# State weights from planes repeated by DMA and formed turned on VectorE, in place of transposes on TensorE

## The chip, the cores and the metric

The kernel runs on one core of one Trainium2 chip. The metric is the time of one execution in microseconds of the device; lower is better. Times are given as the median of several runs; a profiled execution gives the span from the first to the last instruction.

## The reference, cut to what matters

The layer normalises x (512 tokens, 1024 channels), multiplies it by one wide matrix (8192 columns are used here in the parts u, z, q, k, v and two gates), runs a state-space branch (S5) and an attention branch, and merges them. The change is in the S5 branch:

```python
dt = jnp.exp(log_dt.astype(f32))[:, None]
mag = jnp.exp(lr * dt)
ab_re = mag * jnp.cos(li * dt)
ab_im = mag * jnp.sin(li * dt)
den = lr * lr + li * li
nr = ab_re - 1.0
f_re = (nr * lr + ab_im * li) / den
f_im = (ab_im * lr - nr * li) / den
bb_re = f_re[..., None] * br - f_im[..., None] * bi
bb_im = f_re[..., None] * bi + f_im[..., None] * br
...
    bu_re = jnp.einsum('blgp,gnp->blgn', u_c, bb_re)
    bu_im = jnp.einsum('blgp,gnp->blgn', u_c, bb_im)
    pa_re, pa_im, hs_re, hs_im = lax.associative_scan(
        _complex_diag_combine, (a_re, a_im, bu_re, bu_im), axis=1)
```

There are 64 groups with 64 states (n) and 16 channels (p, called q in the kernel). A state is h(t) = a h(t-1) + f b u(t), where a, f and b are complex.

## The kernel before

**Tiling of S5.** The 512 tokens stand as 64 runs of T = 8. For each run and state the kernel needs the sum over the 8 tokens k of a^(7-k) f b u(k). That is a matmul whose contraction goes over the 128 pairs (k, q); its weights W have (k, q) on the partitions and the 64 states of two groups on the columns. Groups are taken in eight batches j of eight groups. W of one batch is 128 x 1024 values: real and imaginary part, eight groups, 64 states.

**How W comes about (lines 434 to 448).** VectorE forms a^k (tile AT) times f b (tile BB) with the states on the partitions, in six operations of 128x512 for each j (`coef`, called twice). Eight transposes of 128x128 on TensorE (`wps`) turn it so that (k, q) lies on the partitions, and two copies of ScalarE bring it from PSUM to W. `x_unit(j)` then multiplies W with the tokens Uj in 32 small matmuls (`xps`) and ScalarE copies the result to Xs.

**Coefficients (lines 514 to 606).** VectorE computes exp, sine and cosine on 64 partitions (groups) with 64 states. Then pw holds the powers a^1 to a^8 and f. `f_turn` turns f by 8 small matmuls (`ftp`) to the layout with states on partitions; GpSimd (into tb) and VectorE make BB = f b from D1, the loaded b. `a_turn` turns the powers by 64 small matmuls (`atp`) into AT.

**After W.** A scan on VectorE runs over the batch results (`scan_work`, tile scn). `ca_coef(j)` forms c a^k on VectorE (six operations of 128x576), `m_unit(j)` multiplies it with BB on TensorE (`kps`), ScalarE copies the result to kt, GpSimd adds the skip and stores kt with eight DMAs in the matrix M. `chunk(j)` computes the output of batch j (`yps` from M, the tokens, the states and ca), then turns it (`yT`) and applies GELU.

**What fills TensorE.** All projections are sums of three matmuls on a high and a low part (`mm3`), in units of 24 matmuls of 128x512 (`cm_unit`, tile pj). Weights are loaded on SyncE's queue, split by ScalarE (w_hi) and VectorE (w_lo).

**What sets the order.** TensorE's instructions have the order in which the program calls them (`follow`, lines 62 to 74). The other engines' order is made by a scheduler of the compiler from a timeline that it simulates, in which an instruction may be placed ahead of others that the program names earlier; `tc.issue_after(ins)` holds an instruction behind another on its engine. The S5 work is placed between projection matmuls by a list of events (lines 939 to 954): each has a block number, and a block is six projection matmuls. Blocks 0 to 19 are the units u(3) to u(7), 20 to 35 za, 36 to 67 zs, then v0, v, rs and ra up to 119.

```python
W0, K0B, V0B, Y0 = 16, 49, 74, 88
```

**Rooms.** Big tiles share places by a tag: s1 is dd (D1, BB and the three M), s5 is abt (the products of `coef`), s6a and s6b the two W, s7a and s7b pw and tq, later kt.

Of the kernel before, what the change touches and what calls it, by code (L numbers as in the profile page):

```python
# [52 lines left out]
def tile_hybrid_block(ctx: ExitStack, tc: tile.TileContext, x, positions, norm_w, w_in, lam_re, lam_im,  # L53
# [382 lines left out]

    def w_unit(j):
        ba = ab[j % 2][:, 0:8 * T * Q].rearrange("p (a g k q) -> p a g k q", a=2, g=4, k=T)
        p4 = slice(4 * j, 4 * j + 4)
        for a in range(2):  # L440
            coef(ba[:, a], 4 * j, BB[:, 1 + a, p4], BB[:, a, p4], 1, T + 1, ab[2][:, 512 * a:], dve)
        W = big.tile([P, 8, P], F32, name="W", tag=("s6a", "s6b")[j % 2])
        for h in range(2):
# [3 lines left out]
            act.copy(W[:, 4 * h:4 * h + 4].rearrange("p g n -> p (g n)"), ps)
        return W
# [98 lines left out]
    dve.tensor_tensor(pw[:, 1, 8], t1, den, op=ALU.mult)
    tq = big.tile([G, 2, 4, N], F32, name="tq", tag="s7b")
    for n in (1, 2, 4):

        br_ = pw[:, 0:1, n - 1:n, :].broadcast_to([G, 2, n, N])
# [4 lines left out]
        dve.tensor_tensor(tq[:, :, 0:n], a, bi_, op=ALU.mult)
# [22 lines left out]
    tb = ab[0][:, 0:1024].rearrange("p (a g q) -> p a g q", a=2, g=H)  # L579
    def f_turn():  # L580
        pf = bank("ftp")
        for i in range(2):
            for h in range(2):
                pe.matmul(pf[64 * h:64 * h + 64, i * H:(i + 1) * H], pw[:, i, 8], idg[:, h], start=True, stop=True,
                          skip_group_check=True)
        act.copy(fT.rearrange("p a g -> p (a g)"), pf[:, 0:2 * H])
        pool.tensor_tensor(tb, D1, fi, op=ALU.mult)
        dve.tensor_tensor(BB[:, 1:3], D1, fr, op=ALU.mult)
        dve.tensor_tensor(BB[:, 2], BB[:, 2], tb[:, 0], op=ALU.add)
        dve.tensor_tensor(BB[:, 1], BB[:, 1], tb[:, 1], op=ALU.subtract)  # L590
        act.activation(BB[:, 0], BB[:, 2], AF.Copy, scale=-1.0)

    def a_turn():
        ps = bank("atp")
        for i in range(2):
            for k in range(8):
# [799 lines left out]
```

## Time and profile before

| | before |
|---|---|
| median of 3 runs | 679.34 us (678.24 to 680.03) |
| profiled execution, its time | 678.55 us |
| its span | 676.5 us |
| granted clock of TensorE | 1.000 |
| DMA packets and bytes | 137380, 82.13 MB |

The page gives, for each engine, the busy time, its share of the span and the number of instructions. Waits are given as engine, line and tile that waited, then what released it, the total in us, how many times, and the longest. The timeline gives start, duration, engine, line, operation, what is written and read, and a count where equal instructions were merged; the duration of a merged row is that of the whole group. In groups of instructions the numbers behind the first bar are the busy sum in us and the mean of one in ns.

### The profile page before, as it was taken

The numbers are of one execution on the slowest core, as the hardware profiler recorded it, in microseconds if no ns is written. First come the engines' busy times: TensorE is split into PE (matmuls) and PEld (weight loads), VectorE is DVE, ScalarE is ACT, GpSimd is POOL, SyncE is SP. The second block draws the span as 40 slices with busy tenths as digits, with TensorE's granted clock in tenths as the row PEclk, the third lists the DMA queues.
The fourth block names the chain that finished last, engine by engine and source line by source line (L and its number), as shares of the span: only waits on it lengthen the run. The fifth ranks groups of instructions, "written<-read, shape, count | busy, mean of one in ns | idle before, by whom it ended". The sixth has DMA issues, their size and how long they took to land.

```text
span 676.5 us, 12719 instructions
## 1 busy us (share of the span) xinstructions
PE 669.5 (99%) x4841; PEld 565.3 (84%) x4841; DVE 465.3 (69%) x964; ACT 322.5 (48%) x677; POOL 118.2 (17%) x274
## 2 busy tenths in 40 slices
PE   8999999999999999999999999999999999999997
PEld 7988888889888888878889888888888888888886
DVE  7989879999788365863238777658566856667531
ACT  6644552423467663431344674557456745633210
POOL 1020000600365329510000030012001200220000
PEclk9999999999999999999999999999999999999999
DMA  9665425552566543573332423222222213237231
GB/s 307 134 164 146 122 55 146 148 167 85 156 141 147 148 148 107 155 249 94 93 107 81 140 63 95 62 63 74 84 83 74 72 55 94 94 134 286 94 125 62
DMA packets 137380, 82.13 MB, mean 121 GB/s; under 512 B 32736, under 2 KB 125928, under 8 KB 137192
## 3 DMA queue, kind: packets, MB, share of 16 engines
q1 hardware_dynamic: 134968, 78.31, 39.2%
q0 software_dynamic: 2048, 2.36, 2.2%
q8 instruction: 38, 0.62, 0.4%
q10 hardware_dynamic: 304, 0.66, 0.3%
q14 instruction: 22, 0.18, 0.1%
HBM read 68.46 MB, written 10.49 MB: 117 GB/s over the span
## 4 chain that ended last, share of the span: by engine, by line
PE 92%; DVE 4%; issue 2%; ACT 1%; DMA 1%; POOL 0%; ACTq 0%; DVEq 0%; POOLq 0%
PE pj L69 76%; PE sps L69 3%; PE yps L69 2%; PE ot L69 2%; PE ptp L74 2%; PE qtp L74 2%; PE xps L69 1%; DVE gth L1258 1%; DVE w_lo L252 1%; PE wps L74 1%; ACT w_hi L250 1%; DMA x_all<-in_x_dram 1%; PE kps L69 1%; PE yT L74 1%; PE cps L69 0%
## 5 line engine op out<-in xcount | busy, mean ns | idle before, releaser
L250 ACT ACTIVATE w_hi<-w_raw 128x1024 fp32r<-128x1024 f32 x94 | 99.4, 1059 | 162.0 <-PE pj L69 132.2
L252 DVE TENSOR_TENSOR w_lo<-w_raw,w_hi 128x1024 fp32r<-128x1024 f32 x94 | 117.1, 1247 | 66.3 <-ACT w_hi L250 65.3
L69 PE MATMUL pj<-hT_hi,w_hi 128*128 128x512 f32 (+1 forms) x344 | 131.8, 385 | 0.0
L69 PE MATMUL pj<-hT_lo,w_hi 128*128 128x512 f32 (+1 forms) x344 | 128.8, 376 | 0.4 <-DVE hT_lo L355 0.4
L69 PE MATMUL pj<-hT_hi,w_lo 128*128 128x512 f32 (+1 forms) x344 | 126.8, 375 | 0.0
L69 PE MATMUL pj<-w_hi,hT_hi 128*128 128x512 f32 (+1 forms) x288 | 108.7, 377 | 0.0
L69 PE MATMUL pj<-w_hi,hT_lo 128*128 128x512 f32 (+1 forms) x288 | 105.6, 367 | 0.0
L69 PE MATMUL pj<-w_lo,hT_hi 128*128 128x512 f32 (+1 forms) x288 | 105.5, 366 | 0.0
L69 PEld LDWEIGHTS pj<-hT_hi,w_hi 128*128 128x128 f32 x344 | 64.7, 188 | 13.1 <-issue 1.3
L69 PEld LDWEIGHTS pj<-hT_lo,w_hi 128*128 128x128 f32 x344 | 64.8, 188 | 11.1 <-DVE hT_lo L355 0.6
L69 PEld LDWEIGHTS pj<-hT_hi,w_lo 128*128 128x128 f32 x344 | 63.7, 188 | 12.0
L69 PEld LDWEIGHTS pj<-w_hi,hT_lo 128*128 128x128 f32 x288 | 54.3, 189 | 9.1
L69 PEld LDWEIGHTS pj<-w_hi,hT_hi 128*128 128x128 f32 x288 | 54.4, 189 | 8.5 <-issue 0.5
L69 PEld LDWEIGHTS pj<-w_lo,hT_hi 128*128 128x128 f32 x288 | 54.5, 189 | 7.5
L1120 POOL COPY sw<-st 32x4 f32<-32x4 f32 x64 | 11.9, 185 | 175.0 <-ACT Pt L1076 172.2
L1021 DVE SCALAR_TENSOR_TENSOR qkp<-qtp,wcol,qkp 128x512 fp32r<-128x512 f32 (+1 forms) x32 | 23.6, 748 | 25.3 <-ACT qkp L1020 25.2
L1076 ACT ACTIVATE Pt<-Pt,st 128x256 f32<-128x256 f32 (+1 forms) x64 | 30.9, 484 | 19.8 <-DVE st L1074 19.8
L845 POOL DMA_DIRECT2D dd<-kt x64 | 33.8, 536 | 2.4 <-POOL kt L841 2.1
L1020 ACT ACTIVATE qkp<-qtp,wcol 128x512 fp32r<-128x512 f32 (+1 forms) x32 | 21.2, 683 | 23.0 <-PE qtp L74 20.8
L69 PE MATMUL pj<-w_lo,mT_hi 128*128 128x512 f32 (+1 forms) x72 | 26.3, 366 | 0.0
L69 PE MATMUL pj<-w_hi,mT_hi 128*128 128x512 f32 (+1 forms) x72 | 26.3, 366 | 0.0
L69 PE MATMUL pj<-w_hi,mT_lo 128*128 128x512 f32 (+1 forms) x72 | 26.3, 365 | 0.0
(301 smaller groups left out, 1189.6 us busy)
## 6 DMA issues: line engine op xcount, KB each, us to landing
w_raw<-in_w_in_dram SPq DMA_DIRECT2D x36, 512.0 KB
w_raw<-in_w_in_dram SPq DMA_DIRECT2D x112, 128.0 KB
w_raw<-in_w_glu_dram SPq DMA_DIRECT2D x8, 512.0 KB
w_raw<-in_w_ssm_out_dram SPq DMA_DIRECT2D x8, 512.0 KB
w_raw<-in_w_o_dram SPq DMA_DIRECT2D x8, 512.0 KB
w_early<-in_w_in_dram SPq DMA_DIRECT2D x4, 512.0 KB
ud<-uT SPq DMA_DIRECT2D x8, 256.0 KB
uss<-ud SPq DMA_DIRECT2D x8, 256.0 KB
```

The costliest lines, as they stand in the source:

```text
L69: last[0] = nc.tensor.matmul(*a, **k)
L74: last[0] = nc.tensor.transpose(*a, **k)
L250: last_act[0] = act.activation(hi, raw, AF.Copy).ins
L252: dve.tensor_tensor(lo, raw, hi.bitcast(F32), op=ALU.subtract)
L845: pool.dma_start(M[Q * t:Q * t + Q, :, 0:P - Q * t], kt[:, :, t:].rearrange("q g k p -> q g (k p)"))
L1020: act.activation(hi, ps[sl], AF.Copy, scale=w)
L1021: dve.scalar_tensor_tensor(lo, ps[sl], w, hi.bitcast(F32), op0=ALU.mult, op1=ALU.subtract)
L1076: act.activation(o, o, AF.Exp, bias=nm, scale=-1.0, accum_out=st[:, kind, 1, h, b:b + 1])
L1120: pool.tensor_copy(sw[32 * r:32 * r + 32, :, :, b], st[32 * b:32 * b + 32, 1, :, :, r])
L1258: dve.scalar_tensor_tensor(th, th, 1.0, z, op0=ALU.add, op1=ALU.mult)
```

## The change

W is no longer turned on TensorE. The products a^(7-k) f are formed on 64 partitions (tile pf, eight rows k), stored to DRAM (pfd), and read back so that each row k of a batch, 1024 values in 4 KB, is repeated on the 16 partitions of its q. b is turned once by eight transposes (`b_turn`), stored (btd), and read back with each row q repeated for the 8 rows k. Both planes then lie as W does, and `w_unit` is four operations of VectorE: two of 128x1024 and two of 128x512. All these DMAs are issued on GpSimd's queue: two stores, and sixteen loads of 512 KB. `f_turn` also turns a; `a_powers` forms the powers with states on the partitions on VectorE, and `a_turn` goes. tb is made on VectorE in place of GpSimd. BB loses its third, negated part. The planes lie in parts of abt and dd, two sets. The two old events of w and x work are parted: `w_next(j)` from block 12 on, `x_unit(j)` from block 15 on, both 3.5 blocks apart. `ca_coef(2)` moves from block 41 to 90, behind the scan. The first chunk moves from block 88 to 90, and chunks are 10/3 in place of 11/3 blocks apart.

```diff
+    def load_planes(j):
+        PB = planes[j % 2]
+        pool.dma_start(PB[0], bass.AP(pfd.tensor, pfd.offset + 1024 * j, [(2 * G * N, T), (0, Q), (1, 1024)]))
+        pool.dma_start(PB[1], bass.AP(btd.tensor, btd.offset + 1024 * j, [(0, T), (2 * H * P, Q), (1, 1024)]))
+        PBs[j] = PB
+
     def w_unit(j):
-        ba = ab[j % 2][:, 0:8 * T * Q].rearrange("p (a g k q) -> p a g k q", a=2, g=4, k=T)
-        p4 = slice(4 * j, 4 * j + 4)
-        for a in range(2):
-            coef(ba[:, a], 4 * j, BB[:, 1 + a, p4], BB[:, a, p4], 1, T + 1, ab[2][:, 512 * a:], dve)
+        PB = PBs.pop(j)
         W = big.tile([P, 8, P], F32, name="W", tag=("s6a", "s6b")[j % 2])
-        for h in range(2):
-            ps = bank("wps")
-            for g in range(4):
-                pe.transpose(ps[:, g * P:(g + 1) * P], ba[:, h, g].rearrange("p k q -> p (k q)"), ident)
-            act.copy(W[:, 4 * h:4 * h + 4].rearrange("p g n -> p (g n)"), ps)
+        Wv = W.rearrange("p m n -> p (m n)").rearrange("p (a g n) -> p a g n", a=2, n=N)
+        pl = PB[0].rearrange("p (g a n) -> p a g n", a=2, n=N)
+        bl = PB[1].rearrange("p (a g n) -> p a g n", a=2, n=N)
+        br, bi = (bl[:, i:i + 1].broadcast_to([P, 2, 8, N]) for i in range(2))
+        dve.tensor_tensor(Wv, pl, br, op=ALU.mult)
+        dve.tensor_tensor(pl, pl, bi, op=ALU.mult)
+        dve.tensor_tensor(Wv[:, 0], Wv[:, 0], pl[:, 1], op=ALU.subtract)
+        dve.tensor_tensor(Wv[:, 1], Wv[:, 1], pl[:, 0], op=ALU.add)
+        if j + 2 < 8:
+            load_planes(j + 2)
         return W
...
-    W0, K0B, V0B, Y0 = 16, 49, 74, 88
+    W0, K0B, V0B, Y0 = 16, 49, 74, 90
...
+    def times(o, a, br_, bi_, t):
         dve.tensor_tensor(o, a, br_, op=ALU.mult)
-        dve.tensor_tensor(tq[:, :, 0:n], a, bi_, op=ALU.mult)
...
+        dve.tensor_tensor(t, a, bi_, op=ALU.mult)
+        dve.tensor_tensor(o[:, 0], o[:, 0], t[:, 1], op=ALU.subtract)
+        done[0] = dve.tensor_tensor(o[:, 1], o[:, 1], t[:, 0], op=ALU.add).ins
+
+    done = [None]
+    tq = big.tile([G, 2, T - 1, N], F32, name="tq", tag="s6b")
+    for n, m in ((1, 1), (2, 2), (4, 3)):
+        e = T - 1
+        sh = [G, 2, m, N]
+        times(pw[:, :, e - n - m:e - n], pw[:, :, e - m:e], pw[:, 0:1, e - n:e - n + 1].broadcast_to(sh),
+              pw[:, 1:2, e - n:e - n + 1].broadcast_to(sh), tq[:, :, 0:m])
+    sh = [G, 2, T - 1, N]
+    times(pf[:, :, 0:T - 1], pw[:, :, 0:T - 1], f1[:, 0:1].unsqueeze(2).broadcast_to(sh),
+          f1[:, 1:2].unsqueeze(2).broadcast_to(sh), tq)
+    pf_done = done[0]
+    pfd = dram.tile([T, G, 2 * N], F32, name="pfd")
+    pool.dma_start(pfd.rearrange("k g m -> g k m"), pft.rearrange("g k a n -> g k (a n)"))
...
-    tb = ab[0][:, 0:1024].rearrange("p (a g q) -> p a g q", a=2, g=H)
+    tb = dd[:, 1024:2048].rearrange("p (a g q) -> p a g q", a=2, g=H)
+    planes = [(abt[:, 3072:4096], dd[:, 2048:3072]), (dd[:, 0:1024], dd[:, 1024:2048])]
...
+    def b_order():
+        for i in range(2):
+            act.copy(dd[:, 1024 + 512 * i:1536 + 512 * i].rearrange("p (m j q) -> p m j q", m=4, q=Q),
+                     D1[:, i].rearrange("p (j m) q -> p m j q", m=4))
+
+    def b_turn():
+        bt = dd[:, 2048:3072]
+        for i in range(2):
+            ps = bank("btp")
+            Dv = dd[:, 1024 + 512 * i:1536 + 512 * i].rearrange("p (m c) -> p m c", m=4)
+            for m in range(4):
+                pe.transpose(ps[:, m * P:(m + 1) * P], Dv[:, m], ident)
+            act.copy(bt[:, 512 * i:512 * i + 512], ps)
+        pool.dma_start(btd.rearrange("q j e -> j q e"), bt)
+
     def f_turn():
...
+        for i, t in enumerate((f1, a1)):
+            for a in range(2):
                 for h in range(2):
...
+        act.copy(fT.rearrange("p a g -> p (a g)"), pf_[:, 0:2 * H])
+        act.copy(AT[:, :, :, T - 1], pf_[:, 2 * H:4 * H].rearrange("p (a g) -> p a g", a=2))
+        with tc.issue_after(pf_done):
+            dve.tensor_tensor(tb, D1, fi, op=ALU.mult)
+        with tc.issue_after(pf_done):
+            dve.tensor_tensor(BB, D1, fr, op=ALU.mult)
...
+    def a_powers():
+        tv = t2k("tv")[:, 0:8 * H].rearrange("p (a g k) -> p a g k", a=2, g=H)
+        for n in (1, 2, 4):
+            sh = [P, 2, H, n]
+            with tc.issue_after(pf_done):
+                times(AT[:, :, :, T - 2 * n:T - n], AT[:, :, :, T - n:T], AT[:, 0:1, :, T - n:T - n + 1].broadcast_to(sh),
+                      AT[:, 1:2, :, T - n:T - n + 1].broadcast_to(sh), tv[:, :, :, 0:n])
...
-    events = [(3, begin_x), (6, lambda: early.update({3: load_u(3, sza[:, 3])})), (8, f_turn), (10, a_turn)]
-    events += [(W0 + 3 * j, lambda j=j: wx(j)) for j in range(8)] + [(W0 + 23, lambda: wx(8))]
+    events = [(3, begin_x), (6, lambda: early.update({3: load_u(3, sza[:, 3])})), (0, b_order), (2, b_turn), (5, f_turn), (6, a_powers)]
+    events += [(6, lambda: load_planes(0)), (6, lambda: load_planes(1))]
+    events += [(12 + 7 * j // 2, lambda j=j: w_next(j)) for j in range(8)]
+    events += [(15 + 7 * j // 2, lambda j=j: x_unit(j, Ws.pop(j))) for j in range(8)]
...
-                   (W0 + 25, lambda j=j: ca_coef(j))]
+                   (W0 + 25 if j < 2 else Y0, lambda j=j: behind_scan(j) if j == 2 else ca_coef(j))]
...
-    events += [(Y0 + (11 * j + 1) // 3, lambda j=j: chunk(j)) for j in range(8)] + [(Y0 + 28, lambda: gelu(7, y_turn(7), *gTs))]
+    events += [(Y0 + (10 * j + 1) // 3, lambda j=j: chunk(j)) for j in range(8)] + [(Y0 + 26, lambda: gelu(7, y_turn(7), *gTs))]
```

More of the change, by code (lines that the diff above doesn't have):

```diff
@@ L578, in tile_hybrid_block @@
     fr, fi = (fT[:, i:i + 1, :].unsqueeze(3).broadcast_to([P, 2, H, Q]) for i in range(2))
-    tb = ab[0][:, 0:1024].rearrange("p (a g q) -> p a g q", a=2, g=H)
-    def f_turn():
[L581 to L596, printed above, removed]
+    tb = dd[:, 1024:2048].rearrange("p (a g q) -> p a g q", a=2, g=H)
+    planes = [(abt[:, 3072:4096], dd[:, 2048:3072]), (dd[:, 0:1024], dd[:, 1024:2048])]
+    PBs = {}
+    btd = dram.tile([Q, 8, 1024], F32, name="btd")
+    def b_order():
+        for i in range(2):
+            act.copy(dd[:, 1024 + 512 * i:1536 + 512 * i].rearrange("p (m j q) -> p m j q", m=4, q=Q),
+                     D1[:, i].rearrange("p (j m) q -> p m j q", m=4))
@@ new lines, in b_turn @@
+    def b_turn():
[7 more added lines that the diff above has]
+        pool.dma_start(btd.rearrange("q j e -> j q e"), bt)
+    def f_turn():
+        pf_ = bank("ftp")
+        for i, t in enumerate((f1, a1)):
+            for a in range(2):
@@ L597, in a_turn @@
                 for h in range(2):
-                    o = i * 8 * H + (7 - k) * H
-                    pe.matmul(ps[64 * h:64 * h + 64, o:o + H], pw[:, i, k], idg[:, h], start=True, stop=True,
+                    o = (2 * i + a) * H
+                    pe.matmul(pf_[64 * h:64 * h + 64, o:o + H], t[:, a], idg[:, h], start=True, stop=True,
                               skip_group_check=True)
-        for i in range(2):
-            act.copy(AT[:, i, :, 0:8], ps[:, i * 8 * H:(i + 1) * 8 * H].rearrange("p (k g) -> p g k", k=8))
+        act.copy(fT.rearrange("p a g -> p (a g)"), pf_[:, 0:2 * H])
@@ L610, in tile_hybrid_block, with w_next @@
     Ws = {}
-    def wx(j):
-        if j < 8:
-            Ws[j] = w_unit(j)
-            if j not in early:
-                early[j] = load_u(j)
-        if j > 0:
-            x_unit(j - 1, Ws.pop(j - 1))
+    def w_next(j):
+        Ws[j] = w_unit(j)
+        if j not in early:
+            early[j] = load_u(j)
     gd = dram.tile([2, KT, P, S], F32, name="gd")
@@ L750, in step @@
         dve.tensor_tensor(dst, x, tv[:, :, 0], op=ALU.add)
-        dve.tensor_tensor(dst, dst, tv[:, :, 1], op=ALU.add)
+        done[0] = dve.tensor_tensor(dst, dst, tv[:, :, 1], op=ALU.add).ins
     Ev = E.rearrange("p a (g j) -> p a g j", j=NJ)
@@ L928, in chunk, with behind_scan @@
             ca_load(j + 4)
+    def behind_scan(j):
+        with tc.issue_after(done[0]):
+            ca_coef(j)
     def scanning(i, n):
```

36 lines of the change are left out of this document (17 added, 19 removed).

## The prediction

> **What bounds the kernel now.** I read the busy shares first, then the list of waits for TensorE alone.
>
> ```profile
> span 676.5 us, 12719 instructions
> PE 669.5 (99%) x4841; PEld 565.3 (84%) x4841; DVE 465.3 (69%) x964; ACT 322.5 (48%) x677; POOL 118.2 (17%) x274
> PE warm L294 <- POOL ident masks.py:199: 1.6, 1, 1.6
> PE hps L74 <- DVE x_all L336: 1.1, 1, 1.1
> ```
>
> TensorE is busy for 669.5 of 676.5 us, and the two longest of its four listed waits, 1.6 and 1.1 us, lie in the loading of x at the start. Its instructions run in the program's order, so the time is the sum of their pitches plus waits. An edit is worth what it takes from or adds to that row of matmuls, less any wait that it opens. Work on the other engines counts only when it arrives late at a matmul. Busy durations overlap, so I price by the distance between starts, in the timeline of TensorE.
>
> ```profile
> 41.47 0.39 PE L69 MATMUL pj<-hT_hi,w_lo 128*128 128x512 f32 x1
> 41.78 0.42 PE L69 MATMUL ftp<-ident,pw 64*64 64x32 f32 x8
> 42.13 0.50 PE L69 MATMUL pj<-hT_hi,w_hi 128*128 128x512 f32 x1
> 42.47 0.39 PE L69 MATMUL pj<-hT_lo,w_hi 128*128 128x512 f32 x1
> 42.70 0.40 PE L69 MATMUL pj<-hT_hi,w_lo 128*128 128x512 f32 x1
> ...
> 44.77 0.39 PE L69 MATMUL pj<-hT_hi,w_lo 128*128 128x512 f32 x1
> 45.08 2.06 PE L69 MATMUL atp<-ident,pw 64*64 64x32 f32 x64
> 47.07 0.50 PE L69 MATMUL pj<-hT_hi,w_hi 128*128 128x512 f32 x1
> ...
> 55.14 0.39 PE L69 MATMUL pj<-hT_hi,w_lo 128*128 128x512 f32 x1
> 55.37 1.03 PE L74 MATMUL wps<-ident,ab 128*128 128x128 f32 x8
> 56.16 0.48 PE L69 MATMUL pj<-hT_hi,w_hi 128*128 128x512 f32 x1
> 56.47 0.39 PE L69 MATMUL pj<-hT_lo,w_hi 128*128 128x512 f32 x1
> ...
> 60.36 1.03 PE L74 MATMUL wps<-ident,ab 128*128 128x128 f32 x8
> 61.32 1.15 PE L69 MATMUL xps<-sza,W 128*64 128x64 f32 x32
> 62.40 0.50 PE L69 MATMUL pj<-hT_hi,w_hi 128*128 128x512 f32 x1
> ...
> 104.55 0.40 PE L69 MATMUL pj<-hT_hi,w_lo 128*128 128x512 f32 x1
> 104.88 1.15 PE L69 MATMUL xps<-Uj,W 128*64 128x64 f32 x32
> ```
>
> A projection matmul (pj) has a pitch of 0.227 us (42.47 to 42.70), so a block of six is 1.36 us. Around the inserted groups the reader sees 0.31 to 0.34 us in place of 0.23.
>
> **What goes from TensorE and what comes.** In w_unit eight transposes go for each j. Where they stand before xps, they take 0.96 us (60.36 to 61.32), but an xps without them has an entry of 0.33 in place of 0.23 (104.55 to 104.88), so each of seven frees 0.86; the first, alone between projections, frees 0.79 (55.37 to 56.16) and 0.08 behind it: 7 x 0.86 + 0.87 = 6.9 us. In a_turn 64 matmuls go: 1.99 (45.08 to 47.07), 0.08 before (44.77 to 45.08) and 0.11 behind, as behind ftp (42.13 to 42.47): 2.2 us. In f_turn the matmuls become 16 from 8, by 1.99/64 = 0.031 each: 0.25 us more. In b_turn come eight transposes, 0.87 as for the first w_unit. The sum for TensorE is -6.9 - 2.2 + 0.25 + 0.87 = **-8.0 us**, if nothing comes late.
>
> **The front: what can come late.** The same edit moves matmuls forward: f_turn from block 8 to 5, the first x_unit from block 19 to 15, and puts a store, a load and four VectorE operations between the coefficients and that x_unit. Block 0 of the list of events is the start of u_unit(3), which is 48 matmuls before the ftp group: 41.78 - 0.08 - 48 x 0.227 = 30.8 us.
>
> ```profile
> 19.71 1.43 SPq L574 DMA_DIRECT2D dd<-in_b_im_dram x1
> DMA to landing us min/median/max: 1.6/3.4/5.6
> 37.87 1.21 DVE L252 TENSOR_TENSOR w_lo<-w_raw,w_hi 128x1024 fp32r<-128x1024 f32 x1
> L556 DVE TENSOR_TENSOR tq<-pw 64x256 f32<-64x256 f32 x1 | 0.4, 410 | 0.0
> 40.14 0.68 DVE L556 TENSOR_TENSOR tq<-pw 64x512 f32<-64x512 f32 x1
> 40.75 0.21 DVE L547 TENSOR_TENSOR pw<-scr 64x64 f32<-64x64 f32 x1
> 43.95 2.96 DVE L588 TENSOR_TENSOR dd<-dd,fT 128x1024 f32<-128x1024 f32 x1
> ```
>
> b_order and b_turn need D1. Its last load is issued by 21.1 us; with the largest landing in the second row (of the DMAs that touch dd) it is there by 27, and block 2 comes at 33.5. The two copies of ScalarE (0.58 us each, as for L447, below) stand in its idle time. I take 0; if ScalarE has them ahead of the sines, up to 1.1 us would pass on to all that follows.
>
> f_turn at block 5 would start at 30.8 + 5 x 1.36 + 0.87 = 38.5. It needs f1, whose last operation (L547) now ends at 40.96. The order of VectorE there changes little; the doubling step ahead of it shrinks from four powers to three, which saves some 0.3 in two operations. So f1 is there at 40.7 and TensorE waits some **2.2 us**. If w_lo (1.2 us), which stands in that row, falls behind f1, the wait is 1.0; if f1 is late by ScalarE's copies, 3.3.
>
> The chain of the planes runs on from there. After f1: two small operations of the powers (0.5), then the products pf, two of 64x896 and two of 64x448. L556 has 0.68 us for 512 elements and 0.41 for 256, 1.05 ns more for each element, so 1.08 and 0.61, less the 0.07 by which neighbours overlap (w_lo: 1.21 lasts, 1.14 to the next), 1.0 and 0.54: 3.1 us, and pf is done at 44.4. For the DMAs I use the rows of the queues.
>
> ```profile
> q1 hardware_dynamic: 134968, 78.31, 39.2%
> q0 software_dynamic: 2048, 2.36, 2.2%
> dd<-kt POOLq DMA_DIRECT2D x8, 64.0 KB, 2.5
> L845 POOL DMA_DIRECT2D dd<-kt x64 | 33.8, 536 | 2.4 <-POOL kt L841 2.1 <-issue 0.3
> L447 ACT COPY W<-wps 128x512 f32<-128x512 f32 x16 | 8.6, 592 | 10.6 <-PE wps L74 10.6
> L424 DVE TENSOR_TENSOR ab<-ab 128x512 f32<-128x512 f32 x16 | 10.3, 678 | 0.0
> ACT w_hi L250 <- DMA w_raw<-in_w_in_dram: 2.1, 1, 2.1
> ```
>
> GpSimd's queue moved 2.36 MB in 2.2% of 16 engines over 676.5 us, 101 engine-us for a MB; SP's 54. A 512 KB load then keeps 16 engines for 1.8 us (SP's rate) to 3.3 us (GpSimd's, with its small scattered rows), the 256 KB store of pf for half. The fixed part is 2.5 less the 0.4 of a 64 KB transfer, 2.1 us, with the issue (0.54) in it. Long rows speak for the lower end, SP's stream beside it (39.2% of the engines on the mean) for the upper. Store landed: 44.4 + 3.0 to 3.8; first plane landed: 51.3 to 53.6, taken 52. W(0) is four operations, two of 128x1024 (1.21 as w_lo, pitch 1.14) and two of 128x512 (0.68, pitch 0.60): 3.5 us, so 54.9 to 57.1, taken 55.6. VectorE is free for it: from 44.4 it has tb and BB (3.5, without the 2.96 of L588, which ran beside GpSimd's L587), the 12 operations of the powers (about 2.4) and one w_lo, and ends near 51.5. TensorE without a wait would reach x_unit(0) at 30.8 + 15 x 1.36 + 0.87 + 0.79 (f_turn: 0.35 + 0.19 of switching + 0.25) = 52.9. On GpSimd's queue the copies for A4, which wait for the powers (near 50.4), come before the loads in the program; were they before them on the queue too, the first plane would be issued some 2.5 us later than in my sum; I take it that the loads, which can start first, go first. So TensorE is late there by **2.7 us in all**, the 2.2 of f_turn contained (bounds 2.0 and 4.5; with a w_lo in between, 5.5).
>
> On this the Trainium skill, page "DMA: Bandwidth & Descriptors", section "Anatomy of one DMA — SWDGE (gpsimd) path", gives about 2.0 us plus bytes over 436 GB/s for one such DMA; an estimate from that page is 2.6 us for the store and 3.2 for the load, the plane at 50.4, a lag of the 2.2 of f_turn and a time lower by 0.5 than my sum. The Trainium skill also has a rule against the change: page "SBUF — State Buffer", section "SBUF: two separate sides", says that a VectorE instruction in a two-port mode keeps GpSimd from writing descriptors. By the rows here, issues beside VectorE's tensor_tensor took 0.54 us each, so the sum stays.
>
> **The steady part.** From x_unit(j) to x_unit(j+1) are 3.43 blocks, 4.7 us, and 1.3 of xps: 6.0 us. VectorE has in it W (3.5) and the w_lo and silu of 0.86 units (1.14 and 0.60 each, 1.5): 5.0. ScalarE loses 16 copies. Nothing waits on average. A pair of planes is reloaded after W(j) for W(j+2): of the 12.0 us between, W takes 3.5 and other work of VectorE up to 1.75, so 6.8 are there for a pair, which takes 2.1 + 3.6 = 5.7 by SP's rate and 2.1 + 6.6 = 8.7 by GpSimd's. I take the lower, as the rows are 4 KB: no wait. The weight loads on SP's queue share engines with 8.4 MB more; now w_hi waits for a load once, for 2.1 us, so the loads have room, and I take 0.
>
> **The chunk stage.** It moves back by two blocks of projection and its eight chunks stand 3.3 blocks apart in place of 3.7: no matmul more or less. What changes is what must be ready.
>
> ```profile
> 110.33 0.69 DVE L726 COPY scn<-A 128x1024 f32<-128x1024 f32 x1
> 174.62 0.69 DVE L751 TENSOR_TENSOR Xs<-Xs,scn 128x512 f32<-128x512 f32 x1
> 176.56 1.16 PE L69 MATMUL yps<-ab,Xs 64*64 64x64 f32 x64
> 177.65 0.66 PE L69 MATMUL kps<-ab,dd 64*16 64x128 f32 x32
> L423 DVE TENSOR_TENSOR ab<-p,AT 128x576 f32<-128x576 f32 x16 | 12.1, 754 | 1.0 <-ACT p L818 0.7
> ```
>
> The scan ends at 175.3, 1.2 us before its reader. It starts 4.4 us behind the last x_unit (104.88 + 1.08), which comes 8.0 - 2.7 = 5.3 earlier; two of three ca_coef still stand before it, behind W(7), which now can't start before x_unit(5). I keep the distance: scan's end 170.0, against a reader at 176.6 - 5.3 + 2.7 = 174.0. Behind the scan stands ca_coef(2), six of 128x576 (0.70 of pitch) and one w_lo: 5.4, so 175.4; its reader is kps of make_m(2) at 175.1. I put 0 here, with bounds 0 and 3 us (a scan that starts later). For M, the way from kps over ScalarE, GpSimd's 8 issues (8 x 0.54) and landing takes some 10 us; six blocks and a chunk leave 12.5. No wait.
>
> **Rivals.** (1) Nothing comes late: f1 ahead of the w_lo, quick planes. Then -8.0 alone, 671.3. For it: chains of VectorE are reordered anyway; against: L547 at 40.96. (2) The front is late by 4.5 and the chunk stage by 1: -2.5, 676.8. For it: the upper rates, A4 ahead on GpSimd's queue, margins of 0 at kps. (3) Slower than before: the pair of planes comes at GpSimd's rate. 8.7 against 6.8 costs 1.9 in each of three rounds of reload, 5.7, with 4.5 at the front 10.2 against 8.0: +2.2, 681.5. It decides from a pair of some 8.5 us on. Against it: 4 KB rows, and a queue that is idle otherwise. That the change doesn't do what it says (transposes still there) I see no way for.
>
> **Numbers.** The profiled execution took 678.55 us, 2.05 around its span of 676.5, and 0.8 below the median of the runs, 679.34. The sum is -8.0 + 2.7 = -5.3: 673.2 for that execution, **674.0** on the median. Chances: forecast 0.48 (672.5 to 675.5), rival 1 0.22, rival 2 0.20, rival 3 0.10. The range 671.0 to 678.0 holds the first three but for an edge. About 0.3%, 2 us, is what a measurement can tell from no change: faster is 0.48 + 0.22 + 0.13 of rival 2 = 0.83, the same 0.10, slower 0.07.
>
> **What would show it.** TensorE's waits must hold a new one at ftp behind VectorE (2.2 us) and one at the first xps behind VectorE's W (0.5, or up to 3); none at later xps, which would be rival 3; none at kps or yps. No wps or atp in the groups, 8 btp and 16 ftp. TensorE's busy sum should go down by about 8 us. I am wrong if plane loads from issue to landing exceed 8 us a pair, or if the scan starts more than 7 us behind the last xps.

## The result, and the profile after

The kernel before took 679.07 us beside the runs of the change (median of 4), the changed kernel **713.64 us** (708.36 to 720.94, median of 4): 1.0483 times as long, interval 1.0423 to 1.0543. It is slower, where the prediction said 674.0. The profiled execution of the changed kernel was the longest of its four, 720.94 us with a span of 719.2, so its waits lie above those of the others; the ratio leaves it out, and the median of the other three is 712.91 us.

First the page's head (busy time by engine), the granted clock in 40 slices, two queues and the chain that ended last; then the list of waits for TensorE alone (us in all, times, longest).

```profile
span 719.2 us, 12508 instructions
...
PE 675.5 (94%) x4729; PEld 568.4 (79%) x4729; DVE 467.1 (65%) x965; ACT 315.7 (44%) x663; POOL 130.4 (18%) x291
...
PEclk9898698899999999999999999999999999999999
...
q1 hardware_dynamic: 134968, 78.31, 37.8%
q0 software_dynamic: 6752, 11.55, 8.6%
...
PE 80%; DMA 9%; DVE 3%; issue 3%; SPq 3%; ACT 1%; POOL 0%; DVEq 0%; POOLq 0%; ACTq 0%
```

```profile
PE xps L69 <- DVE W L453: 30.4, 6, 14.0
PE pj L69 <- ACT hT_hi L353: 3.2, 1, 3.2
PE ftp L69 <- DVE pf L560: 2.1, 1, 2.1
PE warm L294 <- POOL ident masks.py:199: 1.6, 1, 1.6
PE hps L74 <- DVE x_all L336: 1.4, 1, 1.4
PE xps L69 <- DVE W L454: 0.7, 3, 0.3
PE pj L69 <- DVE hT_lo L355: 0.4, 1, 0.4
```

TensorE has 112 instructions fewer and yet is busy for longer: part of its work ran at half clock. The new waits are those for W at the state products (30.4 and 0.7), 3.2 at the first projections and 2.1 at ftp. None stands at kps or yps. The table by windows shows the clock of each stretch, and that all of the loss lies ahead of 151 us (columns: length, busy time and count of PE, PEld, DVE, ACT, POOL, then granted clock, DMA share, GB/s).

```profile
25.00:31.80 6.80, 6.16 (x28) 6.14 (x29) 5.38 (x23) 3.84 (x10) 1.31 (x3) 0.50 0.60 166
66.00:83.00 17.00, 5.51 (x40) 4.54 (x41) 8.93 (x11) 1.57 (x5) 5.68 (x8) 0.50 0.67 146
83.00:110.00 27.00, 21.76 (x174) 17.06 (x172) 12.57 (x13) 8.41 (x19) 2.55 (x5) 1.00 0.94 181
110.00:151.00 41.00, 29.14 (x221) 22.57 (x222) 27.48 (x37) 9.48 (x30) 4.93 (x7) 0.79 0.67 145
151.00:719.00 568.00, 564.45 (x3968) 475.31 (x3966) 373.76 (x762) 264.70 (x560) 110.69 (x252) 1.00 0.40 116
```

GpSimd's timeline (start, length, instruction, what it had waited for) shows the front, and two rows of the list of DMAs give the KB of each and the median from issue to landing.

```profile
42.22 0.81 POOL L619 DMA_DIRECT2D btd<-dd  x1 [12.76 <-ACT dd L618]
51.35 0.61 POOL L441 DMA_DIRECT2D dd<-btd  x1 [8.31 <-DMA btd<-dd]
51.95 0.74 POOL L580 DMA_DIRECT2D pfd<-pf  x1
61.16 0.63 POOL L440 DMA_DIRECT2D ab<-pfd  x1 [8.47 <-DMA pfd<-pf]
```

```profile
dd<-btd POOLq DMA_DIRECT2D x8, 512.0 KB, 10.9
...
ab<-pfd POOLq DMA_DIRECT2D x4, 512.0 KB, 11.6
```

The store of pf stood behind a load of b's planes, which waited 8.3 us for the store of b's planes. VectorE had pf done only at 50.5 us, so 1.5 us were lost behind that load; the store then took 9 us itself, and the first plane was loaded from 61.2 us on, where the prediction had it landed at 52. Each load took some 11 us.

The weight loads came late as well. In the kernel before, ScalarE's w_hi waits once for one, for 2.1 us; here it waits twice, for 28.1 us:

```profile
ACT w_hi L250 <- DMA w_raw<-in_w_in_dram: 28.1, 2, 16.0
```

VectorE's w_lo waits for w_hi, and operations of W stand behind w_lo in VectorE's order: of the 30.4 us of waits for W, 20.8 stand behind planes, 7.7 behind such a w_lo and 1.9 behind other work of VectorE.

### The profile page after: what moved, and what is told of

The parts are those of the page before. It is cut to its first block, busy times and chain, and to the rows that moved or that the text cites. A ratio compares the mean times of both kernels' runs of the same rounds, so it can differ in the third digit from the quotient of the medians.

```text
span 719.2 us, 12508 instructions
## 1 busy us (share of the span) xinstructions
PE 675.5 (94%) x4729; PEld 568.4 (79%) x4729; DVE 467.1 (65%) x965; ACT 315.7 (44%) x663; POOL 130.4 (18%) x291
## 4 chain that ended last, share of the span: by engine, by line
PE 80%; DMA 9%; DVE 3%; issue 3%; SPq 3%; ACT 1%; POOL 0%; DVEq 0%; POOLq 0%; ACTq 0%
PE pj L69 68%; DMA ab<-pfd 3%; DMA w_raw<-in_w_in_dram 3%; PE sps L69 2%; PE yps L69 2%; PE ot L69 2%; PE ptp L74 2%; PE qtp L74 1%; DMA dd<-btd 1%; DMA btd<-dd 1%; SPq L596 1%; DVE w_lo L252 1%; PE kps L69 1%; DMA dd<-in_b_im_dram 1%; SPq L210 1%
## 5 line engine op out<-in xcount | busy, mean ns | idle before, releaser
L69 PE MATMUL pj<-hT_hi,w_hi 128*128 128x512 f32 (+1 forms) x344 | 136.2, 398 | 3.2 <-ACT hT_hi L353 3.2
L69 PE MATMUL pj<-hT_lo,w_hi 128*128 128x512 f32 (+1 forms) x344 | 133.1, 389 | 0.4 <-DVE hT_lo L355 0.4
L69 PE MATMUL pj<-hT_hi,w_lo 128*128 128x512 f32 (+1 forms) x344 | 130.7, 387 | 0.0
L69 PEld LDWEIGHTS pj<-hT_hi,w_hi 128*128 128x128 f32 x344 | 68.1, 198 | 17.3 <-ACT hT_hi L353 3.4
L69 PEld LDWEIGHTS pj<-hT_lo,w_hi 128*128 128x128 f32 x344 | 67.9, 197 | 11.8 <-DVE hT_lo L355 0.6
L69 PEld LDWEIGHTS pj<-hT_hi,w_lo 128*128 128x128 f32 x344 | 66.9, 197 | 12.6
L1065 ACT ACTIVATE qkp<-qtp,wcol 128x512 fp32r<-128x512 f32 (+1 forms) x32 | 21.2, 682 | 23.1 <-PE qtp L74 20.8
L69 PE MATMUL pj<-w_lo,mT_hi 128*128 128x512 f32 (+1 forms) x72 | 26.3, 366 | 0.0
L69 PE MATMUL pj<-w_hi,mT_hi 128*128 128x512 f32 (+1 forms) x72 | 26.3, 366 | 0.0
L69 PE MATMUL pj<-w_hi,mT_lo 128*128 128x512 f32 (+1 forms) x72 | 26.3, 365 | 0.0
## 6 DMA issues: line engine op xcount, KB each, us to landing
dd<-btd POOLq DMA_DIRECT2D x8, 512.0 KB, 10.9
```

Of the source, the lines that this page charges most:

```text
L69: last[0] = nc.tensor.matmul(*a, **k)
L1065: act.activation(hi, ps[sl], AF.Copy, scale=w)
```

## The experiments

They take the change apart, from the back to the front. Times are medians, ratios are to the kernel before on the same chip; the runs stand on several chips.

**The chunk stage alone** (e3_chunk): the kernel before, with Y0 at 90, eight chunks 10/3 blocks apart and the third set of coefficients behind the scan.

```
-    W0, K0B, V0B, Y0 = 16, 49, 74, 88
+    W0, K0B, V0B, Y0 = 16, 49, 74, 90
-    events += [(Y0 + (11 * j + 1) // 3, lambda j=j: chunk(j)) for j in range(8)] + ...
+    events += [(Y0 + (10 * j + 1) // 3, lambda j=j: chunk(j)) for j in range(8)] + ...
```

> The kernel before with the chunk stage's edits alone: first chunk at block 90, chunks 10/3 blocks apart, ca_coef(2) behind the scan. If the chunk stage of the change costs nothing, within 1 us of before. If its closer chunks or ca_coef(2) behind the scan make TensorE wait, 2 to 5 us more, with waits at kps or yps; here the scan starts 4 us earlier than in before, since ca_coef(2) is gone from ahead of it.

Measured: 677.94 us, ratio 0.9986 (0.9977 to 0.9995), no wait at kps or yps. The chunk stage is not the loss; it even gives some 0.9 us.

**b_order behind the first splits** (e1_border): ScalarE's copies held behind hT_hi.

```
+            with tc.issue_after(hi_done):
                 act.copy(dd[:, 1024 + 512 * i:1536 + 512 * i]..., D1[:, i]...)
```

> The changed kernel with one edit: the two ScalarE copies of b_order are held behind the last hT_hi copy. In the changed kernel these copies stand ahead of hT_hi and wait for b, and TensorE waits 3.2 us, with 6.8 us at half clock behind it. If that is a cost of its own, the wait at hT_hi goes and the time falls by 4 to 8 us. If the planes' chain hides it (the first xps waits until the planes land, whenever TensorE comes), TensorE comes earlier and waits longer at the first xps: the time falls by less than 2 us. The chain starts from the coefficients on VectorE, which wait for the same place, so I expect the first.

Measured: 713.14 us, ratio 1.0514 (1.0492 to 1.0537). ScalarE's timeline of the changed kernel shows what this undoes: the copies stand ahead of hT_hi and wait for the load of b (in brackets, us and releaser).

```profile
23.03 0.62 ACT L608 COPY dd<-dd 128x512 f32<-128x512 f32 x1 [3.65 <-DMA dd<-in_b_re_dram]
24.59 0.62 ACT L608 COPY dd<-dd 128x512 f32<-128x512 f32 x1 [0.95 <-DMA dd<-in_b_im_dram]
25.12 3.18 ACT L353 ACTIVATE hT_hi<-hps,nwc 128x256 fp32r<-128x256 f32 x8
```

In e1_border the wait at hT_hi is gone and ftp waits 0.7 in place of 2.1, but the time stays where it was, against the expectation of 4 to 8 us less: the state products still wait 30.1 us for W. As the times of the change spread from 708 to 721 us, a few us either way can't be told. The kernels below are built on this one, but for the loads measured without a layer and c4_powers and c5_early.

**No reload** (e2_noreload): the planes of batches 0 and 1 serve all eight, and the other six pairs are not loaded.

```
-            load_planes(j + 2)
+            PBs[j + 2] = PB
```

> As e1_border, and the planes are loaded for batches 0 and 1 only; batches 2 to 7 use them again, so that W is wrong from batch 2 on, with the same operations on all engines. If the reload of planes is what the later xps wait for, all waits at xps but the first go, with the half clock behind them: 14 to 20 us less than e1_border. If VectorE is the bound in that stage, the waits stay within 3 us of those of e1_border. What is left against the kernel before is then the wait at the first xps, some 10 us, less the 8 us of matmuls saved: 679 to 688.

Measured: 687.24 us, ratio 1.0126 (1.0110 to 1.0141). The waits of TensorE for W shrink to one of 13.5 us. So the six reloaded pairs cost 713.14 - 687.24 = **25.9 us**, more than the 14 to 20 expected.

**The half clock** (e5_fill): in e2_noreload, 116 transposes of the identity fill that one wait.

```
+        if j == 0:
+            fl = bank("fil")
+            for _ in range(116):
+                pe.transpose(fl[:, 0:P], ident, ident)
         ps = bank("xps")
```

> e2_noreload with 116 transposes of the identity on TensorE ahead of the first state products (12.8 us at 0.110 us each), inside the wait of 13.5 us. Theory that idleness halves the granted clock and that this costs time of its own: the halved stretch of 13.65 us goes, TensorE's 5.3 us of work behind the wait run at full pitch, and the time falls by 2.7 us, from 687.2 to 684.5 us. Theory that the halved stretch is only a record beside the wait: 687 us or above, as the transposes are only added work.

Measured: 684.94 us, 2.3 us less with 116 instructions more. The same window of both traces, first e2_noreload, then e5_fill:

```profile
59.20:72.80 13.60, 5.09 (x39) 4.21 (x40) 9.96 (x15) 1.79 (x6) 1.82 (x4) 0.50 0.83 199
```

```profile
59.20:72.80 13.60, 11.37 (x113) 10.50 (x112) 7.72 (x13) 1.42 (x5) 1.82 (x4) 1.00 0.84 162
```

With TensorE kept busy the clock stays at 1.0. Without the filling it is half from 59.2 to 72.8 us, and the 5.3 us of work behind the wait, which ends at 67.5, pay for it.

**No load of planes at all** (e6_ready, then e7_held): all batches read two planes filled with one at the start; both stores to DRAM stay.

```
+    pool.memset(abt[:, 0:2048], 1.0)
...
-        PB = planes[j % 2]
-        pool.dma_start(PB[0], ...)
-        pool.dma_start(PB[1], ...)
+        PB = (abt[:, 0:1024], abt[:, 1024:2048])
```

> e1_border with no load of planes at all: all eight batches read two planes set to one by a fill at the start (the state weights are wrong), both stores to DRAM stay. If the sum of TensorE's work in the prediction (8.0 us less) was right and the loads of the planes are all that went wrong: no wait at the state products, clock 1.0 throughout, 670.5 to 672 us. If another part of the change costs time that the waits hide: 674 to 680 us.

Measured: 675.52 us, ratio 0.9948 (0.9931 to 0.9965), the second of the two expectations. In part this is the edit's own doing: with the planes ready from the start, W(0) stood on VectorE at 16.9 us among the norms of x, and the transposes of x waited 2.5 us. In e7_held VectorE's four operations of W are held behind pf.

```
+        with tc.issue_after(pf_done):
+            dve.tensor_tensor(Wv, pl, br, op=ALU.mult)
             ...
```

> e6_ready with the state weights held on VectorE behind the end of pf, as the true data would hold them, so that the first of them no longer stands among the early norms (where it cost 2.5 us at the transposes of x, 3.4 us at half clock and 1.6 us at the state products). If the sum of 8.0 us was right: no wait at hps or xps, clock 1.0, 670.5 to 672 us. If more than the planes' loads was wrong: 674 us and above.

Measured: 678.77 us, ratio 0.9992 (0.9978 to 1.0005), again the second expectation. TensorE waits 5.3 us at the first state products although no plane is loaded. VectorE's timeline says why:

```profile
47.03 1.22 DVE L450 TENSOR_TENSOR W<-ab 128x1024 f32<-128x1024 f32 x1
...
50.76 1.22 DVE L451 TENSOR_TENSOR ab<-ab 128x1024 f32<-128x1024 f32 x1
56.87 1.22 DVE L252 TENSOR_TENSOR w_lo<-w_raw,w_hi 128x1024 fp32r<-128x1024 f32 x1 [4.89 <-ACT w_hi L250]
...
58.43 0.68 DVE L452 TENSOR_TENSOR W<-W,ab 128x512 f32<-128x512 f32 x1
```

The last two operations of W(0) stand behind a w_lo that waits for its weights. Their load was late on SyncE's queue; first that queue in the kernel before, then in e7_held:

```profile
36.88 2.47 SPq L409 DMA_DIRECT2D sza<-ud  x2
39.45 1.50 SPq L435 DMA_DIRECT2D ud<-uT  x1
41.04 0.41 SPq L210 DMA_DIRECT2D w_raw<-in_w_in_dram  x1
```

```profile
37.44 8.00 SPq L409 DMA_DIRECT2D sza<-ud  x2
45.53 1.70 SPq L435 DMA_DIRECT2D ud<-uT  x1
47.33 0.41 SPq L210 DMA_DIRECT2D w_raw<-in_w_in_dram  x1
```

A reload of sza waits for the store of ud ahead of it, which ran beside GpSimd's 512 KB store of b's planes (35.8 to 45.5 us); the weight load behind it is issued 6.3 us late.

**Without that store** (e8_nostore): e7_held less one line.

```
-        pool.dma_start(btd.rearrange("q j e -> j q e"), bt)
```

> e7_held without the store of b's planes to DRAM (they are not read there). In e7_held the 512 KB store ran from 35.8 to 45.5 us, SyncE's load of sza behind it took 8.0 us to issue where it took 2.5 before, the next weight load was issued at 47.3 where it was 41.0, its split on VectorE waited 4.9 us, and the first state weights stood behind that split. If the store's company on the DMA engines is what delays SyncE's queue: the weight load is issued near 41 us, no wait of 5.3 us at the state products, clock 1.0, and 670.5 to 672.5 us. If the delay is the order on VectorE alone: 677 us as in e7_held.

Measured: **671.51 us**, ratio 0.9902 (0.9885 to 0.9919), clock 1.0, no wait at the state products above 0.3 us, the weight load issued at 41.76. The store cost 678.77 - 671.51 = **7.3 us** (6.1 by the two ratios) through SyncE's queue, and with the loads of planes and this store gone the sum for TensorE stands (below).

**What makes a load slow.** m1_dma runs the DMAs without a layer, four of each kind.

> No layer is computed: only 512 KB DMAs, one after the other, four of each kind, with nothing beside them; the output is zeros. In the changed kernel a plane load takes 9.2 to 11.9 us from issue to landing. Theory queue (GpSimd's queue is slow by itself for 128 rows of 4 KB): all loads on GpSimd's queue land in 8 us or more, rows repeated or not, and the same loads on SP's queue in under 5. Theory source (a few 4 KB rows, 32 KB apart, read by all engines at once): repeated rows land in 8 us or more on both queues, 128 different rows in under 5 on both. Theory company (SP's weight stream and a second plane beside it): every load lands in under 6 here, and the pair in under 8. By the Trainium skill's page DMA: Bandwidth & Descriptors, an estimate of 2.0 us plus bytes over 436 GB/s gives 3.2 us for each on GpSimd's queue.

The medians from issue to landing, from the trace's view of each line: 6.3 us for 8 rows each 16 times and 6.6 for 16 rows 8 times, 3.6 for 128 different rows, 6.7 for repeated rows 4 KB apart and not 32, 6.0 for the store of b's planes. The first two kinds had loads of a second tile beside them, which the compiler had moved forward; 8 rows each 16 times without that took 6.0. None of the three theories was met in its figures (8 us or more, or under 6 throughout), but on SyncE's queue the distances between loads were 6.3 and 3.2 us, so the queue isn't it: the pattern of rows is. In the kernel (e4_rows) the reloads then took 128 different rows, which are not those that W needs:

```
+        if j > 1:
+            for b in PB:
+                pool.dma_start(b, bass.AP(btd.tensor, btd.offset, [(1024, P), (1, 1024)]))
```

> e1_border with the loads of planes 2 to 7 reading 128 different 4 KB rows in the place of 8 or 16 rows repeated; the state weights of batches 2 to 7 are then wrong. If the repeated rows are what makes the reloads late (6.3 us against 3.6 us alone), four loads need 14.4 us where two units give 13.6 us: waits at the state products after the first fall from some 17 us to 0 to 5 us and the time to 688 to 695 us. If it is the company on the DMA engines, the loads still take 9 us and more and the time stays at 705 to 713 us.

Measured: 692.87 us, ratio 1.0221 (1.0197 to 1.0244); 15.8 us of waits at the state products, 13.0 of them the first. The median landing of the reloads falls from some 11 us to 6.5 and 8.0 for the two planes. So of the 25.9 us some 20 go with the repeated rows; the other 5.6 stay with different rows. Next, which repetition is slow (m2_rows):

> No layer is computed: only 512 KB loads into 128 rows of 4 KB on GpSimd's queue, four of each kind, one after the other: 1, 2, 4, 32 and 64 different rows of DRAM, each repeated side by side; 4 and 32 rows repeated in turn; 128 rows of SBUF; 16 rows of SBUF taken eight times by eight loads. If it is the small number of places in DRAM that makes repeated rows slow (6.3 us for 8 and 16 rows, 3.6 us for 128): 1 to 4 rows take longer than 6.3 us, 32 and 64 rows lie between 3.6 and 6.3 us, SBUF takes about 3.6 us. If any repetition costs the same: 6.3 us for all of them.

Neither theory held: 64 rows each twice running were quick and 2 rows slow, but 32 rows in turn were slow too (table below). The order on the partitions counts, not the repetition. e9_order loads the change's rows in the other order (the state weights' rows are then permuted):

```
-        [(2 * G * N, T), (0, Q), (1, 1024)]
+        [(0, Q), (2 * G * N, T), (1, 1024)]
-        [(0, T), (2 * H * P, Q), (1, 1024)]
+        [(2 * H * P, Q), (0, T), (1, 1024)]
```

> e1_border with the same planes, rows and bytes loaded in another order of the 128 partitions: f's eight rows in turn (16 times over) in place of each 16 times running, b's sixteen rows each 8 times running in place of in turn. The rows of the state weights then do not stand as the inputs' rows do, so the result is not the layer's. By m2_rows, where 4 rows in turn took 3.5 us and 32 rows each four times running 3.6 us, but 4 rows each 32 times running 8.4 us and 32 rows in turn 8.5 us, it is which partitions share a row that matters: then the loads are as quick as those of different rows, 690 to 695 us as e4_rows. If repeating eight or sixteen rows is slow in either order: 711 to 715 us.

Measured: 698.76 us, ratio 1.0299 (1.0282 to 1.0316): 14.4 us less than e1_border, between the two expectations and nearer to that of quick loads. What is left is mostly not the planes: 18.0 of the 20.9 us of waits for W stand behind a w_lo on VectorE whose weights were late. First ScalarE's waits, then such a w_lo and the wait of 8.4 us behind it:

```profile
ACT w_hi L250 <- DMA w_raw<-in_w_in_dram: 36.5, 5, 19.7
```

```profile
110.88 1.23 DVE L252 TENSOR_TENSOR w_lo<-w_raw,w_hi 128x1024 fp32r<-128x1024 f32 x1 [12.22 <-ACT w_hi L250]
...
116.08 2.16 PE L69 MATMUL xps<-Uj,W 128*64 128x64 f32 x32 [8.38 <-DVE W L453]
```

m3_order shows these loads by themselves:

> No layer is computed: 512 KB loads alone on GpSimd's queue, four of each kind: 8, 16, 2 and 64 rows of DRAM in turn (32 KB apart), then 16 rows each 8 times running and 8 rows each 16 times running (32 KB apart), 16 rows 4 KB apart each 8 times running, and 8 rows 36 KB apart each 16 times running. The orders of e9_order are the first and the fifth. If the gain of 14.4 us in e9_order comes from the loads themselves: both take about 3.6 us where the change's orders (16 in turn, 8 running) take 6.3 to 6.5 us. If it comes from what the loads meet in the kernel: 6 us in every order. Rows 36 KB apart take 6.3 us if the distance of the rows plays no part.

GpSimd's timeline of m3_order, the first of four loads of each kind (8, 16, 2, 64 rows in turn; 16, 8 rows running; 16 rows 4 KB apart running). Each load is issued when the one before it has landed, so a quarter of the way to the next row is the time of one:

```profile
1.26 0.67 POOL L29 DMA_DIRECT2D A<-in_w_in_dram  x1 [0.81 <-PEq L62]
...
20.30 0.60 POOL L29 DMA_DIRECT2D A<-in_w_in_dram  x1 [4.32 <-DMA A<-in_w_in_dram]
...
46.81 0.59 POOL L29 DMA_DIRECT2D A<-in_w_in_dram  x1 [6.00 <-DMA A<-in_w_in_dram]
...
63.72 0.82 POOL L29 DMA_DIRECT2D A<-in_w_in_dram  x1 [3.34 <-DMA A<-in_w_in_dram]
...
115.83 0.52 POOL L32 DMA_DIRECT2D A<-in_w_in_dram  x1 [12.55 <-DMA A<-in_w_in_dram]
...
134.26 0.59 POOL L32 DMA_DIRECT2D A<-in_w_in_dram  x1 [4.12 <-DMA A<-in_w_in_dram]
...
160.72 0.52 POOL L34 DMA_DIRECT2D A<-in_w_in_dram  x1 [5.76 <-DMA A<-in_w_in_dram]
```

With the same reading of m2_rows:

| 512 KB load, us from issue to issue | 2 | 4 | 8 | 16 | 32 | 64 |
|---|---|---|---|---|---|---|
| first number in the load's list of dimensions | 64 | 32 | 16 | 8 | 4 | 2 |
| a row stands on so many partitions running | 4.5 | 4.1 | 4.6 | 6.6 | 9.1 | 12.9 |
| the rows come again after so many partitions | 4.2 | 4.0 | 4.8 | 6.6 | 9.1 | 13.0 |

The change has f's rows 16 partitions running and b's coming again after 16: 6.6 in both. e9_order has 8 and 8: 4.6 and 4.8. The distance of the rows in DRAM plays no part (4.6 at 4 KB; 6.6 at 36 KB for 8 rows each 16 times).

Why a run or a period of 16 and more is slow no run settles, but the runs order the cases. The two lines of times agree because the time goes by the first number in the list of dimensions in the program: 4.0 to 4.8 us from 16 on, 6.6 at 8, 9.1 at 4, 13 at 2. One row on all 128 partitions, whose first dimension is 1 and whose second is 128, took 4.3. The change's loads begin with 8, as does the store of b's planes; those of e9_order begin with 16. The table by windows shows the share of the 16 DMA engines (the last figure but one) while loads ran that begin with 2 (m2_rows), then with 8 (m3_order):

```profile
18.60:70.10 51.50, 0.00 (x0) 3.16 (x5) 1.00 0.14 41
```

```profile
20.30:46.80 26.50, 0.00 (x0) 2.35 (x4) 1.00 0.31 79
```

That is 2.2 and 5.0 of 16 engines; it is 3.0 at 4 (share 0.19) and 6.6 at 16 (0.41). So it looks as if a load is dealt to about as many DMA engines as its first number says, up to 16. That is inferred from these shares, which hold the idle time between loads too; no run shows the engines one by one.

**All of it together, with the layer computed** (c6_all): e9_order, a second copy of u in DRAM in the planes' order, b's planes turned at block 0 and stored row after row, f's store no longer behind a waiting load, the state products and the scan two blocks later.

```
+        act.dma_start(ux[j].rearrange("g q s c -> (g q) (s c)"), uT)
-        pool.dma_start(btd.rearrange("q j e -> j q e"), bt)
+        pool.dma_start(btd.rearrange("j q e -> (j q) e"), bt)
+        with tc.issue_after(pf_done):
+            pool.dma_start(PB[0], ...)
-    events += [(15 + 7 * j // 2, lambda j=j: x_unit(j, Ws.pop(j))) for j in range(8)]
+    events += [(17 + 7 * j // 2, lambda j=j: x_unit(j, Ws.pop(j))) for j in range(8)]
```

> The change with what the runs before showed put right, and the layer computed: planes' rows in the order of e9_order (and a second copy of u in DRAM, stored by ScalarE's queue, whose rows stand in the same order), b's planes turned at block 0 instead of 2 and stored row after row, their first load ahead of and f's store no longer behind a load that waits, the state products two blocks later (and the scan behind them two blocks later, closer together). If the loads' order and the two stores make up the 36.7 us of waits and 14.0 us at half clock: waits of at most 5 us in all and 672 to 679 us. If four loads of 512 KB for two batches still don't fit beside SyncE's stream (9.7, 2.6 and 8.4 us of waits in e9_order): 685 to 697 us.

Measured: 690.53 us, ratio 1.0173 (1.0156 to 1.0190): the second theory. The store of b's planes now lands in 5.1 us, that of pf in 5.3, and the profiled execution (688.59) has 9.7 us left of waits at one line of W (and 1.1 at the next):

```profile
PE xps L69 <- DVE W L466: 9.7, 3, 5.9
```

```profile
dd<-btd POOLq DMA_DIRECT2D x8, 512.0 KB, 7.8
ab<-pfd POOLq DMA_DIRECT2D x4, 512.0 KB, 6.6
dd<-pfd POOLq DMA_DIRECT2D x4, 512.0 KB, 7.1
```

A load that takes under 5 us alone takes 6.6 to 7.8 beside SyncE's stream. But of the 9.7 us only 3.5 are a wait for a plane, the first. The longest, 5.9, is none: the first operation of W(4) starts to read both its planes at 83.6 us, and the second stands behind a w_lo whose weights were late on SyncE's queue:

```profile
83.57 1.23 DVE L464 TENSOR_TENSOR W<-ab,dd 128x1024 f32<-128x1024 f32 x1 [1.63 <-DMA ab<-pfd]
90.83 1.22 DVE L252 TENSOR_TENSOR w_lo<-w_raw,w_hi 128x1024 fp32r<-128x1024 f32 x1 [6.04 <-ACT w_hi L250]
```

No run moved that w_lo behind W, so what this would win is open.

**What can be kept** (c4_powers, c5_early): the kernel before with the chunk stage of e3_chunk, and of the rest only that the powers of the transition come from one turned value.

```
-        ps = bank("atp")
-        for i in range(2):
-            for k in range(8):
-                ...pe.matmul(ps[...], pw[:, i, k], idg[:, h], ...)
+        pf = turned(0)
+        act.copy(AT[:, :, :, T - 1], pf[:, 0:2 * H].rearrange("p (a g) -> p a g", a=2))
+        for n in (1, 2, 4):
+            times(AT[:, :, :, T - 2 * n:T - n], AT[:, :, :, T - n:T], ...)
```

> The kernel before with the chunk stage of e3_chunk, and with the powers of the transition made on VectorE from one turned value (the change's a_powers) where 32 products on TensorE turned all eight; the state weights are formed as before. TensorE's sum: 2.2 us less for the products that go, 0.25 us more for four more at ftp, 1.1 us less as in e3_chunk: 676.0 us. If the powers on VectorE come late for the first state weights: a wait at wps and 678 to 681 us.

Measured: 681.21 us, ratio 1.0035 (1.0023 to 1.0048), as the second expectation had it: 3.1 us of wait at wps, as the powers stood behind the 2.96 us product of f_turn on VectorE, and 3.4 us at half clock.

> c4_powers with the first power turned by TensorE at block 5 in place of 10, ahead of f_turn, so that the powers on VectorE (3.4 us) run in its idle 4.2 us before 43 us and not behind the 2.96 us product of f_turn. If the lateness of the powers made the 3.1 us wait at wps and the 3.4 us at half clock behind it: no wait, 676 us. If the three more instructions for each power are too much for VectorE anywhere ahead of the first coefficients: 678 us and above.

Measured: 677.60 us, ratio 0.9977 (0.9967 to 0.9987), where 676 was expected. It is 1.4 us faster than the kernel before, but by no more than e3_chunk alone (677.94) within what these runs can tell; waits of 0.5 us each at wps and yps take part of the 2.0 us back.

## Why the prediction was wrong

The way from 678.9 to 713.6 us, from pairs of runs. The second, fourth and last pair differ by one edit; the third differs also in the planes' filling and in the hold on W. The pairs stand on different chips, so the last column gives the same step by the ratios to the kernel before.

| Step | Runs | us, medians | us, ratios |
|---|---|---|---|
| TensorE's instructions, chunk stage | before to e8_nostore | -7.4 | -6.7 |
| store of b's planes | e8_nostore to e7_held | +7.3 | +6.1 |
| first two pairs of planes | e7_held to e2_noreload | +8.5 | +9.1 |
| six pairs reloaded | e2_noreload to e1_border | +25.9 | +26.3 |
| b_order ahead of hT_hi | e1_border to the change | +0.5 | -2.1 |

- **The bound and the sum of -8.0 us: right, to within 1 us.** In e8_nostore the span is 669.8, 6.7 below that of before, with 0.7 us of wait at ftp and 0.6 at the state products in it, which the prediction counted apart: -8.0, of which the chunk stage may have given some tenths.
- **The chunk stage at nothing: right** to 0.9 us (e3_chunk).
- **b_order at 0: wrong, its weight not told.** The prediction had the copies in ScalarE's idle time. They stood ahead of hT_hi on its queue and held the first projections for 3.2 us; in e1_border, without that wait, the first plane was loaded 7.3 us earlier in the profiled execution (53.9 in place of 61.2), yet the time was the same within its spread. Why the gain got lost was not shown.
- **f_turn, 2.2 us: 2.1 measured, by luck.** f1 and TensorE were both some 6 us late there. In e1_border, where the front came near the forecast, f1 was there at 39.5 in place of 40.7 and the wait was 0.7. pf done at 44.4: in e1_border VectorE's last operation of it ends at 44.5, which is right; in the change it ends at 50.5.
- **"Store landed: 44.4 + 3.0 to 3.8": the first step that failed.** Without the planes' transfers that store lands in 3.2 us (e8_nostore). In e1_border it stood 2.2 us behind a load which waited for the store of b's planes, and then took 6.9; in the change it was 1.5 and 8.9. The prediction named A4's copies as what could stand ahead on GpSimd's queue and never asked what a waiting load holds up. It gave the 512 KB store of b's planes no price, neither its own time nor what it does to SyncE's queue: 7.3 us.
- **"A pair takes 5.7 to 8.7 us, I take the lower": the step that cost most.** The fixed 2.1 and the rate were taken from the averages of two queues. One load took 10.9 us at the median, not 3.9. The order of its rows on the partitions makes 6.6 of it, which no row of before could show; the rest comes in company, of SyncE's stream and of the other planes, which no run parts. The estimate of 3.2 us from the Trainium skill, page "DMA: Bandwidth & Descriptors", section "Anatomy of one DMA — SWDGE (gpsimd) path", is nearly met by 128 different rows (3.6) and missed by these. The plane that the prediction put at 50.4 by this estimate would by its own terms, 44.4 + 2.6 + 3.2, come at 50.2.
- **"So the loads have room, and I take 0": wrong.** The prediction gave SyncE's weight loads no delay from 8.4 MB more. From 55 to 75 us the DMA engines were busy for 0.60 of the time in before and 0.92 in the change, w_hi waited 28.1 us for weights in place of 2.1, and W then stood behind w_lo. What this alone costs was measured only for the store of b's planes.
- **Half clock: not in the sum at all.** TensorE's clock is 1.0 throughout in before, so nothing there showed it. Behind the 13.5 us wait it cost 2.3 us (e5_fill).
- **Rival 3 had the mechanism**: pairs of planes later than the room of 6.8 us for them. Its price, 5.7 us for the reloads and 4.5 for the front, was mis-sized against 25.9 and 15.8, as its upper end was again an average of the queue. "Plane loads over 8 us a pair" was rightly named as what would prove the forecast wrong.

## What to carry to other kernels

A transfer that is new on a path must be priced by one like it: same pattern on the partitions, same company, and what stands in the queue behind it when it waits. An average of a queue is not such a price. Ask as well what stands behind a late load on an engine that works in order: here W stood behind the split of late weights. Where the work taken from the busiest engine is 8 us, 8 us are the most that the change can win, while each new dependency can cost its full lateness and a stretch at half clock behind it.

## What the runs showed of the hardware

- **A repeated row of DRAM is not slow by itself.** A 512 KB load of 4 KB rows took 4.0 to 4.8 us where a row ran over, or came again after, up to 8 partitions, 6.6 at 16 and 13 at 64, but 4.3 for one row on all 128; 128 different rows took 3.6 to 3.9. The first number in the list of dimensions orders all of them: 16 and more was quick, 8, 4 and 2 slow in turn.
- **A wait of 2 to 3 us can halve TensorE's clock behind it.** The window table has stretches at a granted clock of 0.50 that last 3.4 us or a multiple: 6.8 us (25.0 to 31.8) at a wait of 3.2 that ends at 25.6, and in e2_noreload 13.6 us (59.2 to 72.8) at a wait of 13.5 that ends at 67.5, so that 8.3 of them lie in the wait. The Trainium skill, page "TensorE: Matmul & The Clock Gate", section "HAM oscillation — how this bites in real kernels", sets the limit at gaps of some 3.4 us; behind the 2.1 us wait at ftp, which ends at 47.3 us, the changed kernel already has one halved window, with TensorE busy all through that window. Filling a wait with transposes kept the clock at 1.0 and won 2.3 us.

```profile
48.85:52.26 3.41, 3.41 (x10) 2.64 (x9) 3.38 (x5) 0.00 (x0) 0.91 (x2) 0.50 0.56 132
```

- **A store on GpSimd's queue delays SyncE's.** One 512 KB store of 9.7 us made SyncE's next weight load 6.3 us late, through a load that waits for a store.
